# Attention probabilities and values in float32r parts, gates applied by diagonal matrices in the transposes

## The chip, the core and the metric

The kernel runs on one NeuronCore of one Trainium2 chip. TensorE (PE) multiplies, VectorE (DVE), ScalarE (ACT) and GpSimd (POOL) work element by element, and the SyncE queue (SP) issues nearly all transfers. The metric is the device time of one execution in microseconds; less is better.

## What is computed

One layer of a decoder trunk on 512 tokens of 1024 features: RMS norm, one input projection, three groups of heads side by side (six gated DeltaNet heads, six sparse attention heads, a causal pooling), an output projection with a residual, then a squared-ReLU MLP with a residual. The change lies in the sparse attention. Cut to what matters:

```
s   = einsum(q, k)                         # 6 heads, 2 key/value groups, blocks of 128 queries
p_c = masked_softmax(s_cmp);  o_c = p_c @ vc      # compressed keys
o_s = masked_softmax(s_sel) @ vsel                # selected blocks: here all causal keys
o_w = masked_softmax(s_win) @ vwb                 # window of 512: here all causal keys
out = g[..., 0] * o_c + g[..., 1] * o_s + g[..., 2] * o_w
```

With 512 tokens the selection takes every block and the window reaches back over everything, so both branches are plain causal attention with keys and values of their own.

## The kernel before, in words

The program has three stretches. Up to about 245 us, slabs of the input projection run beside the DeltaNet solves and scans. From about 247 to 370 us the attention (`attentions`, L1140) runs beside the first parts of the output projection (`out_gdn`). Then come the last part of the output projection with the second norm (`out_tile`, `x2_norm`, `x2_T`) and the MLP to the end at 732 us.

A Python list of generators (`side_by_side`, L1222) sets the order in which work is written down, and a scheduler that models times orders it again on each engine; the engines then run in that order.

One *unit* of the attention is one head and one of two branches, so there are 12. `probs` (L1092) makes, for each block of 128 queries, the scores: two products of float32r parts (L1100, L1101) and a mask product (L1102); DVE takes the row maximum (L1104), ACT the exponential with its row sum (L1106). When the four blocks are done, DVE makes gate over sum (L1109, L1110) and the four tiles of probabilities are multiplied by it: three on DVE (L1115), the widest on ACT (L1113). `values` (L1117) transposes the ten causal 128 by 128 blocks on PE (L1124) in three groups of four, four and two, copies each group out of PSUM (ACT L1129, DVE L1127 for the second) and multiplies it by the values (L1135), which have 64 columns, in plain float32. A pair of heads shares one PSUM bank: the even head has partitions 0 to 63, the odd one 64 to 127. The compressed branch adds one product per head (L1155). `finish` (L1161) splits the bank into the float32r parts `yTh` and `yTl` (`split_rows`, ACT L148 and DVE L149).

`out_tile` multiplies three products of parts per chunk of features (`mm3`, L143 to L145); each is float32r, 128 by 128 by 512. Its weights are loaded and split into parts by ACT and DVE (`load_wo`, L134 and L135). Chunks 6, 7 and then 0, 1, 2 run beside the attention; 3, 4, 5 (the attention's own) come after it.

`x2_T` (L1247), after the attention, already transposes by a plain float32 product with a diagonal matrix: 4 blocks of tokens by 8 chunks, 32 products.

Of the kernel before, what the change touches and what calls it, by code (L numbers as in the profile page):

```python
# [37 lines left out]
def trunk_kernel(ctx, tc, x, norm_mix, w_in, conv_w, a_log, dt_bias, gdn_norm, nsa_q_norm, nsa_k_norm,  # L38
# [14 lines left out]
    def nm(s):  # L53
        _n[0] += 1
        return f"{s}{_n[0]}"
# [22 lines left out]
    N2 = 25  # L78

    def t2(shape, name, dt=F32):  # L80
        return r2.tile(shape, dt, tag="t", name=nm(name), bufs=N2)

# [307 lines left out]
    halves = [slice(0, 64), slice(64, 128)]  # L390

    XT, Vt = {}, {}
    VC = ctile([96, 2, HD], F32, "VC")
    KCT = ctile([P, 2, 64], F32R, "KCT")
    kr = gdp.tile([P, NT, H, HD], F32, tag="kr", name="kr")
    qr = gdp.tile([P, NT, H, HD], F32, tag="qr", name="qr")
# [186 lines left out]
    def compress_half(a, q):  # L583
# [25 lines left out]
        if a == 0:  # L609
            kp = acc[:, 384:448]  # L610
            for m in range(2):
                PE.matmul(kp[0:64, 0:HD], hh[:, ts(m, 64)], w2[:, m, :], start=(m == 0), stop=(m == 1))
            kcs = cmp_.tile([64, HD], F32, tag="kcs", name=nm("kcs"))
            ss = sml.tile([P, 1], F32, tag="ss1", name=nm("ss"))
            r = sml.tile([P, 1], F32, tag="r1", name=nm("r"))
            S.activation(kcs, kp[0:64, 0:HD], AF.Square, accum_out=ss[0:64])
            V.tensor_scalar(ss[0:64], ss[0:64], 0.5 / HD, 0.5 * EPS, ALU.mult, ALU.add)
            rsqrt(r[0:64], ss[0:64], 1, 64)
            V.scalar_tensor_tensor(kcs, kp[0:64, 0:HD], r[0:64], gk_b[0:64, 0, :], ALU.mult, ALU.mult)
            kx = cmp_.tile([64, 2, P], F32, tag="hid", name=nm("kx"))  # L620
            S.copy(kx[:, 0, 0:HD].bitcast(F32R), kcs)
            S.copy(kx[:, 0, HD:P].bitcast(F32R), kcs)
            V.tensor_tensor(kx[:, 1, 0:HD], kcs, kx[:, 0, 0:HD], ALU.subtract)
            V.tensor_tensor(kx[:, 1, HD:P], kcs, kx[:, 0, 0:HD], ALU.subtract)
            kq = acc[:, 0:128]
            for b in range(2):
                PE.transpose(kq[:, ts(b, 64)], kx[:, b, :], ident[:64, :64])
            S.copy(KCT.rearrange("p k (b n) -> p b k n", b=2), kq[:, 0:128].rearrange("p (b k n) -> p b k n", b=2, k=2))
        else:
            vp = acc[:, 384:512]  # L630
            for rep in range(3):
                for kv in range(2):
# [3 lines left out]
            S.copy(VC, vp[0:96, 0:128].rearrange("p (k d) -> p k d", k=2))  # L636


    PW = ctile([P, 2, P], F32, "PW")
# [41 lines left out]
                G.tensor_tensor(z3, z3, gnh.unsqueeze(1).to_broadcast([P, n // HD, HD]), ALU.mult)  # L681

    def vcopy(b0, pss):
        for b in range(2):
            if b not in Vt:
                Vt[b] = t2([P, 2, 4, HD], "Vt")
            S.copy(Vt[b][:, :, b0:b0 + 2, :], pss[b][:, :, 0:128].rearrange("p i (k d) -> p i k d", k=2))

    def conv_slab(cols):
        fs = {"q": 0, "k": 384, "v": 768, "u": 2718}  # L690
# [354 lines left out]
    wr = ctx.enter_context(pool("wr", 2, side="right"))  # L1045
    nwe = ExitStack()
    nw = nwe.enter_context(pool("nw", 2, side="right"))
    wop = [nwe.enter_context(pool(f"wo{n}", n, side="right")) for n in (4, 6)]
    gd.close()
    fe = ExitStack()  # L1050
    wq = fe.enter_context(pool("wq", 2))


    pn, pt_, pa = banks(0, 1), banks(2, 6), banks(7)

    def cmp_probs(kv):

# [28 lines left out]
        pt = nw.tile([96, T], F32, tag=f"pcT{kv}", bufs=1, name=nm("pcT"))  # L1086
        S.copy(pt, tp[0:96])
        return pt

    BLKS = ([(0, i) for i in range(4)], [(1, i) for i in range(1, 4)] + [(3, 3)], [(2, 2), (2, 3)])  # L1090

    def probs(h, br, out):  # L1092

        kv = h // 3
        kb = 6 + 4 * br + 2 * kv
# [12 lines left out]
            yield 0.11 * (i + 1)  # L1108
        V.reciprocal(sm, sm)  # L1109
        V.tensor_tensor(sm, sm, gate[:, :, 3 * h + 1 + br], ALU.mult)  # L1110
        for i in range(NT):
            if i == 3:
                S.mul(out[i], out[i], sm[:, i:i + 1])  # L1113
            else:
                V.tensor_scalar(out[i], out[i], sm[:, i:i + 1], None, ALU.mult)  # L1115

    def values(acc, h, br, Ps):  # L1117

        a = h % 2
        for b, blks in enumerate(BLKS):  # L1120
            n = len(blks) * P
            tp = pt_()
            for c, (k, i) in enumerate(blks):
                PE.transpose(tp[:, ts(c, P)], Ps[i][:, ts(k, P)], ident)  # L1124
            pt = nw.tile([P, n], F32, tag=f"pt{b}", name=nm("pt"))
            if b == 1:
                V.tensor_copy(pt, tp[:, :n])  # L1127
            else:
                S.copy(pt, tp[:, :n])  # L1129
            yield 0.4  # L1130
            c = 0
            while c < len(blks):
                k, i = blks[c]
                m = sum(1 for x_ in blks if x_[0] == k)
                PE.matmul(acc[halves[a], i * P:(i + m) * P], Vt[k // 2][:, k % 2, 2 * br + h // 3, :],  # L1135
                          pt[:, c * P:(c + m) * P], start=False, stop=(br == 1 and k == 2), skip_group_check=True)
                c += m
            yield 0.4

    def attentions():  # L1140
        last = iter(())
        for pr in range(3):
            hd = (2 * pr, 2 * pr + 1)
            for h in hd:
                if h % 3 == 0:
                    pcT[h // 3] = cmp_probs(h // 3)
            acc = pa()
            for br in range(2):
                for h in hd:
                    Ps = []  # L1150
                    yield from in_turn((probs(h, br, Ps), last))
                    if br == 0 and h == hd[0]:
                        for a, h_ in enumerate(hd):
                            r = slice(32 * (h_ % 3), 32 * (h_ % 3) + 32)
                            PE.matmul(acc[halves[a]], VC[r, h_ // 3], pcT[h_ // 3][r], start=True, stop=False,  # L1155
                                      skip_group_check=True)
                    last = values(acc, h, br, Ps)
                    if br == 1 and h == hd[1]:
                        last = finish(last, pr, acc)
        yield from last  # L1160

    def finish(gen, pr, acc):
        yield from gen
        y_tiles((3 + pr,))
        split_rows(yTh[3 + pr], yTl[3 + pr], acc)
        have.add(("y", 3 + pr))

    pcT = {}


    wo = {}
# [233 lines left out]
```

## Time and profile before

| | us |
|---|---|
| median of 3 runs | 734.62 (733.9 to 736.54) |
| profiled execution, its own time | 734.32 |
| its span in the trace | 732.5 |

A row of the trace gives an instruction's start and how long it was under way. A matmul's row includes its way through the array, which overlaps the next one: what one costs PE is the distance from its start to the start of the next.

### The profile page before, as it was taken

The page shows a single profiled execution, that of the slowest core. Times are in us where ns is not written, and L with a number is a line of the kernel's source. Part 1 is how long each engine was busy: PE and PEld are TensorE (multiplying, and loading weights), DVE is VectorE, ACT ScalarE, POOL GpSimd, SP SyncE. Part 2 cuts the span into 40 slices and gives each one's busy share as a digit, 9 for nine tenths or more (in the row PEclk, how much of TensorE's full clock was granted, in tenths as well). Part 3 has the DMA queues.
Part 4 walks back from the last instruction along what each step waited for, and adds up shares of the span by engine and source line. Part 5 has one row for each costly group of instructions (what it writes and reads, how often), then busy time and mean ns, then how long its engine had stood idle before and what let it go on. Part 6 is the DMA issues. An engine that isn't in the chain of part 4 may idle for free.

```text
span 732.5 us, 13228 instructions
## 1 busy us (share of the span) xinstructions
PE 709.9 (97%) x5147; PEld 567.7 (77%) x5147; DVE 550.1 (75%) x1046; ACT 369.4 (50%) x728; POOL 170.1 (23%) x256
## 2 busy tenths in 40 slices
PE   8999999998999999999999999999999999999997
PEld 6888877886998767666478878888888888888885
DVE  4688998878686588676545798896858688796846
ACT  4456835564663366466525744454544544444430
POOL 5730003312042110000020150404124050403223
PEclk9999999999999999999999999999999999999999
DMA  6233223131410531023001142413142332303103
GB/s 219 60 108 98 75 60 87 31 96 56 118 44 3 214 104 58 2 63 112 0 6 81 58 173 66 165 44 129 58 148 82 115 115 88 133 16 111 58 1 115
DMA packets 49780, 61.67 MB, mean 84 GB/s; under 512 B 5479, under 2 KB 42549, under 8 KB 49718
## 3 DMA queue, kind: packets, MB, share of 16 engines
q1 hardware_dynamic: 48852, 60.64, 26.1%
q8 instruction: 40, 0.66, 0.4%
q10 hardware_dynamic: 866, 0.20, 0.1%
q14 instruction: 22, 0.18, 0.1%
HBM read 58.73 MB, written 2.10 MB: 83 GB/s over the span
## 4 chain that ended last, share of the span: by engine, by line
PE 78%; DVE 13%; issue 2%; ACT 2%; DMA 1%; POOL 1%; SPq 0%; DVEq 0%; ACTq 0%; POOLq 0%
PE ps L143 18%; PE ps L144 18%; PE ps L145 17%; PE ps L429 6%; PE ps L1135 4%; PE ps L800 2%; PE ps L1124 2%; PE ps L1100 1%; PE ps L592 1%; DVE lo L135 1%; PE ps L1101 1%; PE ps L905 1%; DVE bl L1281 1%; DVE lw L135 1%; DMA raw<-in_w_in_dram 1%
## 5 line engine op out<-in xcount | busy, mean ns | idle before, releaser
L144 PE MATMUL ps<-h2l,hw 128*128 128x512 f32 (+1 forms) x280 | 104.7, 375 | 0.1
L145 PE MATMUL ps<-h2h,lw 128*128 128x512 f32 (+1 forms) x280 | 104.3, 374 | 0.0
L143 PE MATMUL ps<-h2h,hw 128*128 128x512 f32 (+1 forms) x280 | 103.8, 374 | 0.0
L143 PE MATMUL ps<-bh,ah 128*128 128x512 f32 x224 | 88.6, 396 | 0.6 <-DVE x L1374 0.6
L1288 POOL TENSOR_TENSOR al<-gF,ah 128x512 fp32r<-128x512 f32 x24 | 37.6, 1568 | 219.3 <-ACT ah L1287 180.2
L144 PE MATMUL ps<-bl,ah 128*128 128x512 f32 x224 | 88.4, 395 | 0.0
L145 PE MATMUL ps<-bh,al 128*128 128x512 f32 x224 | 84.8, 394 | 0.0
L1374 DVE TENSOR_TENSOR x<-ps,x 128x512 f32<-128x512 f32 x112 | 72.5, 680 | 5.8 <-PE ps L145 5.7
L1281 DVE TENSOR_TENSOR bl<-w2r,bh 128x1024 fp32r<-128x1024 f32 x40 | 57.8, 1446 | 6.2 <-ACT bh L1280 6.2
L144 PEld LDWEIGHTS ps<-h2l,hw 128*128 128x128 f32 x280 | 52.6, 188 | 10.3 <-DVE h2l L1252 0.3
L145 PEld LDWEIGHTS ps<-h2h,lw 128*128 128x128 f32 x280 | 52.5, 188 | 10.1
L143 PEld LDWEIGHTS ps<-h2h,hw 128*128 128x128 f32 x280 | 52.2, 188 | 10.1
L1288 POOL TENSOR_TENSOR al<-gS,ah 128x512 fp32r<-128x512 f32 x32 | 53.4, 1685 | 26.0 <-ACT ah L1287 26.0
L135 DVE TENSOR_TENSOR lo<-raw,hi 128x512 fp32r<-128x512 f32 (+1 forms) x76 | 43.3, 593 | 15.5 <-ACT hi L134 11.9
L1280 ACT CAST bh<-w2r 128x1024 fp32r<-128x1024 f32 x40 | 41.7, 1046 | 23.5 <-PE ps L145 23.2
L143 PEld LDWEIGHTS ps<-bh,ah 128*128 128x128 f32 x224 | 42.1, 188 | 11.4 <-ACT ah L1287 0.8
L134 ACT CAST hi<-raw 128x512 fp32r<-128x512 f32 (+1 forms) x76 | 37.0, 518 | 26.8 <-DMA raw<-in_w_in_dram 9.3
L144 PEld LDWEIGHTS ps<-bl,ah 128*128 128x128 f32 x224 | 42.2, 188 | 9.8
L145 PEld LDWEIGHTS ps<-bh,al 128*128 128x128 f32 x224 | 42.1, 188 | 9.9
L135 DVE TENSOR_TENSOR lw<-raw,hw 128x1024 fp32r<-128x1024 f32 x32 | 41.2, 1321 | 6.4 <-ACT hw L134 6.2
L1287 ACT CAST ah<-gS 128x512 fp32r<-128x512 f32 x32 | 19.7, 620 | 51.8 <-DVE gS L1356 24.5
L134 ACT CAST hw<-raw 128x1024 fp32r<-128x1024 f32 x32 | 32.1, 1046 | 24.9 <-PE ps L144 22.6
(364 smaller groups left out, 1674.0 us busy)
## 6 DMA issues: line engine op xcount, KB each, us to landing
raw<-in_w_ffn_dram SPq DMA_DIRECT2D x32, 512.0 KB, 3.8
w2r<-in_w_ffn_dram SPq DMA_DIRECT2D x32, 512.0 KB, 6.4
raw<-in_w_in_dram SPq DMA_DIRECT2D x24, 256.0 KB, 2.9
raw<-in_w_in_dram SPq DMA_DIRECT2D x36, 128.0 KB, 2.5
x<-in_x_dram SPq DMA_DIRECT2D x8, 512.0 KB, 6.0
raw<-in_cmp_w_dram SPq DMA_DIRECT2D x32, 128.0 KB, 2.2
raw<-in_w_out_dram SPq DMA_DIRECT2D x8, 512.0 KB, 4.5
out_dram<-x SPq DMA_DIRECT2D x8, 256.0 KB, 2.0
```

The costliest lines, as they stand in the source:

```text
L134: {"A": S.copy, "V": V.tensor_copy, "G": G.tensor_copy}[e[0]](hi[:, k], r)
L135: {"V": V, "G": G}[e[1]].tensor_tensor(lo[:, k], r, f32v(hi[:, k]), ALU.subtract)
L143: PE.matmul(ps, ah, bh, start=start, stop=False, **kw)
L144: PE.matmul(ps, ah, bl, start=False, stop=False, **kw)
L145: PE.matmul(ps, al, bh, start=False, stop=stop, **kw)
L429: PE.matmul(ps[:, ts(i, 256)], a_[:, k, ts(2 * b + i, P)], w_, start=(k == 0 and n_ == 0 and i == 0), stop=(k == KC - 1 and n_ == 2 and i ...
L1135: PE.matmul(acc[halves[a], i * P:(i + m) * P], Vt[k // 2][:, k % 2, 2 * br + h // 3, :], pt[:, c * P:(c + m) * P], start=False, stop=(br = ...
L1280: S.copy(hi, src)
L1281: V.tensor_tensor(lo, src, f32v(hi), ALU.subtract)
L1287: S.copy(hi, src)
L1288: G.tensor_tensor(lo, src, f32v(hi), ALU.subtract)
L1374: V.tensor_tensor(x2[i][:, cs], acc[bk, t_], x2[i][:, cs], ALU.add)
```

## The change

What it does, part by part:

- Probabilities are no longer multiplied by gate over sum. `probs` makes four diagonal matrices `dg` (ACT, `ident` scaled by `sm`), and the blocks are transposed by a plain float32 product with `dg`, which applies the gate, in place of PE's transposition with `ident`.
- For the first two groups of blocks, probabilities are split into two float32r parts (ACT and DVE), and values are stored as [high | low], 128 columns. Each of the two parts is multiplied by both, so an accumulator has the sum with the high values in partitions 0 to 63 and with the low values in 64 to 127. The third group stays float32 with 64 columns (`Vt[2]`).
- Each head has an accumulator of its own, on banks 7 and 3 in turn. `finish` adds its two halves (ACT copy, DVE addition) and, for the odd head, splits the pair's result from SBUF.
- The compressed values get 128 columns and zero rows for other heads (`VCz`); their probabilities are split too.
- `vcopy` and the compressed values (`VC`) split when they leave PSUM. The pool of common tiles grows from 25 to 27, and the pool `wo6` (weights of chunks 0 to 2) is laid out after the DeltaNet's pool `gd` is closed.

```diff
-    VC = ctile([96, 2, HD], F32, "VC")
+    VC = ctile([96, 2, 2, HD], F32R, "VC")
...
-            S.copy(Vt[b][:, :, b0:b0 + 2, :], pss[b][:, :, 0:128].rearrange("p i (k d) -> p i k d", k=2))
+                S.copy(Vt[i][:, b0:b0 + 2], src)
+            else:
+                split_rows(Vt[i][:, b0:b0 + 2, 0], Vt[i][:, b0:b0 + 2, 1], src)
...
-    wop = [nwe.enter_context(pool(f"wo{n}", n, side="right")) for n in (4, 6)]
+    wop = [nwe.enter_context(pool("wo4", 4, side="right"))]
     gd.close()
+    wop.append(nwe.enter_context(pool("wo6", 6, side="right")))
...
-    pn, pt_, pa = banks(0, 1), banks(2, 6), banks(7)
+    pn, pt_, pa = banks(0, 1), banks(2, 6), banks(7, 3)
...
+        dg = nw.tile([P, NT, P], F32, tag="dgp", name=nm("dg"))
         for i in range(NT):
-            if i == 3:
-                S.mul(out[i], out[i], sm[:, i:i + 1])
-            else:
-                V.tensor_scalar(out[i], out[i], sm[:, i:i + 1], None, ALU.mult)
+            S.activation(dg[:, i], ident, AF.Copy, scale=sm[:, i:i + 1])
+            out[i] = out[i], dg[:, i]
...
-                PE.transpose(tp[:, ts(c, P)], Ps[i][:, ts(k, P)], ident)
-            pt = nw.tile([P, n], F32, tag=f"pt{b}", name=nm("pt"))
-            if b == 1:
-                V.tensor_copy(pt, tp[:, :n])
+                PE.matmul(tp[:, ts(c, P)], Ps[i][0][:, ts(k, P)], Ps[i][1], start=True, stop=True)
+            if b == 2:
+                pt = [nw.tile([P, n], F32, tag=f"pt{b}", name=nm("pt"))]
+                S.copy(pt[0], tp[:, :n])
             else:
-                S.copy(pt, tp[:, :n])
+                pt = [nw.tile([P, n], F32R, tag=f"pt{c}{b}", name=nm("pt")) for c in "hl"]
+                split_rows(pt[0], pt[1], tp[:, :n])
...
-                PE.matmul(acc[halves[a], i * P:(i + m) * P], Vt[k // 2][:, k % 2, 2 * br + h // 3, :],
-                          pt[:, c * P:(c + m) * P], start=False, stop=(br == 1 and k == 2), skip_group_check=True)
+                for p_ in pt:
+                    v_ = Vt[k][:, 2 * br + h // 3]
+                    PE.matmul(acc[0:64 if b == 2 else P, i * P:(i + m) * P],
+                              v_ if b == 2 else v_.rearrange("p c d -> p (c d)"),
+                              p_[:, c * P:(c + m) * P], start=False, stop=(br == 1 and b == 2), skip_group_check=True)
...
+                if br == 0:
+                    for n_, p_ in enumerate(pcT[h // 3]):
+                        PE.matmul(acc, VCz[:, h], p_, start=n_ == 0, stop=False, skip_group_check=True)
...
+        S.copy(o[a], acc[halves[1 - h % 2]])
+        V.tensor_tensor(o[a], acc[a], o[a], ALU.add)
+        if h % 2:
+            y_tiles((3 + h // 2,))
+            split_rows(yTh[3 + h // 2], yTl[3 + h // 2], o)
```

The order moves at three places that matter here. PE, the last unit, before: transposes (`P`), value products (`pt`, `Vt`; output 64 partitions), then the output projection.

```order
L1124 MATMUL ps_5541<-ident,P_5517 128x128 x2
L1135 MATMUL ps_5240<-pt_5538,Vt_4003 64x512
L1124 MATMUL ps_5550<-ident,P_5502 128x128
L1124 MATMUL ps_5550<-ident,P_5517 128x128
L1135 MATMUL ps_5240<-pt_5546,Vt_4003 64x384
L1135 MATMUL ps_5240<-pt_5546,Vt_4005 64x128
L1135 MATMUL ps_5240<-pt_5553,Vt_4005 64x256
L143 MATMUL ps_5576<-hwo_5250,yTh_4993 128x512
```

And now (line numbers are those of the changed kernel, L1130 the transposition by `dg`, L1144 the value product):

```order
L1130 MATMUL ps_5680<-dg_5658,P_5650 128x128 x2
L1144 MATMUL ps_5523<-pt_5674,Vt_4004 128x512
L1144 MATMUL ps_5523<-pt_5675,Vt_4004 128x512
L1144 MATMUL ps_5523<-pt_5685,Vt_4007 128x384
L1130 MATMUL ps_5693<-dg_5658,P_5633 128x128
L1130 MATMUL ps_5693<-dg_5658,P_5650 128x128
L1144 MATMUL ps_5523<-pt_5686,Vt_4007 128x384
L1144 MATMUL ps_5523<-pt_5685,Vt_4012 128x128
L1144 MATMUL ps_5523<-pt_5686,Vt_4012 128x128
L1144 MATMUL ps_5523<-pt_5696,Vt_4010 64x256
L143 MATMUL ps_5721<-hwo_5346,yTh_5018 128x512
```

Three of the value products stand twice, once per part, and only the last has 64 output partitions. In the whole program the visits of PE to value products with 64 output columns (runs of such rows, those of the compressed values included) fall from 29 to 12.

ACT, the end of the attention, before: multiplication of the widest probabilities, two copies, the split of the result.

```order
L1106 ACTIVATE P_5517,sm_5471<-ps_5511,mx_5515 128x512
L1129 COPY pt_5530<-ps_5527 128x256
L1113 ACTIVATE P_5517<-P_5517,sm_5471 128x512
L1129 COPY pt_5538<-ps_5533 128x512
L1129 COPY pt_5553<-ps_5550 128x256
L148 CAST yTh_5556<-ps_5240 128x512
```

And now:

```order
L1112 ACTIVATE P_5650,sm_5599<-ps_5644,mx_5648 128x512
L1133 COPY pt_5666<-ps_5663 128x256
L1119 ACTIVATE dg_5658<-ident,sm_5599 128x128 x4
L148 CAST pt_5674<-ps_5669 128x512
L148 CAST pt_5685<-ps_5680 128x512
L1133 COPY pt_5696<-ps_5693 128x256
L1176 COPY o_5594<-ps_5523 64x512
L148 CAST yTh_5701<-o_5594 128x512
```

Four diagonals stand in place of one wide multiplication, both large groups are cast here, and a copy stands ahead of the result's cast.

ACT, the weights of chunks 0 to 2 (`hwo`) beside the scans (`vb`, whose last row is the scan's last copy), before: the first of the three casts.

```order
L909 COPY vb<-ps_3288 64x3x64 x2
L134 CAST hwo_4826<-raw_4828 128x1024
L1106 ACTIVATE P_4605,sm_4598<-ps_4599,mx_4603 128x128
L1106 ACTIVATE P_4628,sm_4598<-ps_4622,mx_4626 128x256
L1113 ACTIVATE P_4588<-P_4588,sm_4533 128x512
L134 CAST hwo_4832<-raw_4834 128x1024
```

And now, three scan steps later, behind the scan's last copy:

```order
L913 COPY vb<-ps_3408 64x3x64
L1112 ACTIVATE P_4931,sm_4924<-ps_4925,mx_4929 128x128
L923 ACTIVATE sq_4448<-vb 128x384
L1119 ACTIVATE dg_4912<-ident,sm_4816 128x128 x4
L148 CAST yTh_3242<-ps_4378 128x128
L1112 ACTIVATE P_4948,sm_4924<-ps_4942,mx_4946 128x256
L134 CAST hwo_4877<-raw_4879 128x1024
```

These weights now lie where tiles of the scan were, and wait for its end.

## Rows read from the trace of the kernel before

**Rows 1.** Page, parts 1 and 4: busy engines; the last-ending chain by engine.

```profile
PE 709.9 (97%) x5147; PEld 567.7 (77%) x5147; DVE 550.1 (75%) x1046; ACT 369.4 (50%) x728; POOL 170.1 (23%) x256
...
PE 78%; DVE 13%; issue 2%; ACT 2%; DMA 1%; POOL 1%; SPq 0%; DVEq 0%; ACTq 0%; POOLq 0%
```

**Rows 2.** Stretches: length, busy PE, PEld, DVE, ACT, POOL (count), granted clock, DMA.

```profile
247.00:270.00 23.00, 21.79 (x180) 15.01 (x180) 20.59 (x55) 13.21 (x29) 4.62 (x7) 0.93 0.62 223
...
345.00:372.00 27.00, 25.91 (x125) 14.42 (x124) 12.79 (x32) 13.42 (x35) 0.00 (x0) 1.00 0.00 1
355.00:370.00 15.00, 13.91 (x65) 7.16 (x65) 7.25 (x19) 7.59 (x20) 0.00 (x0) 1.00 0.01 2
```

**Rows 3.** PE groups by line and shape, 235 to 380 us.

```profile
L1124 PE MATMUL ps<-ident,P 128*128 128x128 f32 x120 | 19.8, 283 | 0.3 <-ACT pcT L1087 0.2
L1135 PE MATMUL ps<-pt,Vt 128*64 128x512 f32 x24 | 12.9, 618 | 0.4 <-ACT pt L1129 0.3
```

**Rows 4.** Timeline of PE: start, us, engine, line, shape, count.

```profile
351.29 0.28 PE L1101 MATMUL ps<-XT,XT 128*128 128x128 f32 x1
351.40 0.23 PE L1102 MATMUL ps<-negb,identb 128*128 128x128 bf16 x1
...
352.99 0.61 PE L1124 MATMUL ps<-ident,P 128*128 128x128 f32 x4
353.53 0.65 PE L1135 MATMUL ps<-pt,Vt 128*64 128x256 f32 x2
354.11 0.66 PE L1124 MATMUL ps<-ident,P 128*128 128x128 f32 x4
...
354.78 0.34 PE L1101 MATMUL ps<-XT,XT 128*128 128x384 f32 x1
354.95 0.23 PE L1102 MATMUL ps<-negb,identb 128*128 128x128 bf16 x1
355.12 1.07 PE L1135 MATMUL ps<-pt,Vt 128*64 128x512 f32 x2
356.12 0.44 PE L1124 MATMUL ps<-ident,P 128*128 128x128 f32 x2
```

**Rows 5.** Timeline of PE after the attention: output projection, then diagonal products.

```profile
383.24 0.39 PE L145 MATMUL ps<-hwo,yTl 128*128 128x512 f32 x1
383.47 1.95 PE L1247 MATMUL ps<-dg,x 128*128 128x128 f32 x16
385.17 0.48 PE L143 MATMUL ps<-hwo,yTh 128*128 128x512 f32 x1
```

**Rows 6.** Line L1247: count, min/median/max ns.

```profile
L1247 PE MATMUL ps<-dg,x x64: 270/275/377, 383.5 to 401.2; 128*128 128x128 f32 x64
```

**Rows 7.** Timeline: the cast of chunk 2's weights, the compressed values' products.

```profile
265.80 1.05 ACT L134 CAST hwo<-raw 128x1024 fp32r<-128x1024 f32 x1 [0.52 <-DMA raw<-in_w_out_dram]
...
265.91 1.07 PE L1155 MATMUL ps<-pcT,VC 32*64 32x512 f32 x4
```

**Rows 8.** ACT groups, 235 to 380 us.

```profile
L1113 ACT ACTIVATE P<-P,sm 128x512 f32<-128x512 f32 x12 | 8.6, 720 | 2.4 <-DVE sm L1110 2.3
```

**Rows 9.** Timeline of ACT: scaled copies of 128x128.

```profile
384.56 2.17 ACT L1250 ACTIVATE h2h<-ps,vT 128x128 fp32r<-128x128 f32 x8 [2.42 <-PE ps L1247]
```

**Rows 10.** Timeline: the last unit, from gate over sum to the output projection.

```profile
364.12 0.18 DVE L1109 RECIPROCAL sm<-sm 128x4 f32<-128x4 f32 x1 [0.84 <-ACT P L1106]
...
364.53 0.88 DVE L1115 TENSOR_SCALAR P<-P,sm 128x128 f32<-128x128 f32 x3
...
369.54 0.50 PE L143 MATMUL ps<-hwo,yTh 128*128 128x512 f32 x1
...
369.64 0.59 ACT L148 CAST yTh<-ps 128x512 fp32r<-128x512 f32 x1 [1.07 <-PE ps L1135]
...
370.26 0.69 DVE L149 TENSOR_TENSOR yTl<-ps,yTh 128x512 fp32r<-128x512 f32 x1 [3.16 <-ACT yTh L148]
...
371.03 0.40 PE L143 MATMUL ps<-hwo,yTh 128*128 128x512 f32 x1
```

More of the change, by code (lines that the diff above doesn't have):

```diff
@@ L77, in trunk_kernel @@
     r2 = ctx.enter_context(pool("r2", 1))
-    N2 = 25
+    N2 = 27
     def t2(shape, name, dt=F32):
@@ L635, in compress_half @@
                                   w2[:, m, :], start=(m == 0), stop=(m == 1))
-            S.copy(VC, vp[0:96, 0:128].rearrange("p (k d) -> p k d", k=2))
+            split_rows(VC[:, :, 0], VC[:, :, 1], vp[0:96, 0:128].rearrange("p (k d) -> p k d", k=2))
     PW = ctile([P, 2, P], F32, "PW")
@@ L683, in vcopy @@
     def vcopy(b0, pss):
-        for b in range(2):
-            if b not in Vt:
-                Vt[b] = t2([P, 2, 4, HD], "Vt")
-            S.copy(Vt[b][:, :, b0:b0 + 2, :], pss[b][:, :, 0:128].rearrange("p i (k d) -> p i k d", k=2))
+        for i in range(NT):
+            src = pss[i // 2][:, i % 2, 0:128].rearrange("p (k d) -> p k d", k=2)
+            if i not in Vt:
+                Vt[i] = t2([P, 4, HD], "Vt") if i == 2 else t2([P, 4, 2, HD], "Vt", F32R)
+            if i == 2:
+                S.copy(Vt[i][:, b0:b0 + 2], src)
+            else:
+                split_rows(Vt[i][:, b0:b0 + 2, 0], Vt[i][:, b0:b0 + 2, 1], src)
     def conv_slab(cols):
@@ L1085, in cmp_probs @@
             PE.transpose(tp[0:96, ts(i, P)], pc[:, i].rearrange("p g n -> p (g n)"), ident)
-        pt = nw.tile([96, T], F32, tag=f"pcT{kv}", bufs=1, name=nm("pcT"))
-        S.copy(pt, tp[0:96])
+        pt = [nw.tile([96, T], F32R, tag=f"pcT{c}{kv}", bufs=1, name=nm("pcT")) for c in "hl"]
+        split_rows(pt[0], pt[1], tp[0:96])
         return pt
@@ L1110, in probs @@
         V.tensor_tensor(sm, sm, gate[:, :, 3 * h + 1 + br], ALU.mult)
+        dg = nw.tile([P, NT, P], F32, tag="dgp", name=nm("dg"))
         for i in range(NT):
-            if i == 3:
-                S.mul(out[i], out[i], sm[:, i:i + 1])
-            else:
-                V.tensor_scalar(out[i], out[i], sm[:, i:i + 1], None, ALU.mult)
+            S.activation(dg[:, i], ident, AF.Copy, scale=sm[:, i:i + 1])
+            out[i] = out[i], dg[:, i]
     def values(acc, h, br, Ps):
-        a = h % 2
         for b, blks in enumerate(BLKS):
@@ L1140, in attentions, with finish @@
     def attentions():
+        G.memset(f32v(VCz), 0.0)
+        for h in range(H):
+            r = slice(32 * (h % 3), 32 * (h % 3) + 32)
+            S.copy(VCz[r, h], f32v(VC[r, h // 3]).rearrange("p c d -> p (c d)"))
         last = iter(())
[L1142 to L1146, printed above, removed]
+        for h in range(H):
+            if h % 3 == 0:
+                pcT[h // 3] = cmp_probs(h // 3)
             acc = pa()
             for br in range(2):
[L1149 to L1159, printed above, removed]
+                Ps = []
+                yield from in_turn((probs(h, br, Ps), last))
+                if br == 0:
+                    for n_, p_ in enumerate(pcT[h // 3]):
+                        PE.matmul(acc, VCz[:, h], p_, start=n_ == 0, stop=False, skip_group_check=True)
+                last = values(acc, h, br, Ps)
+            last = finish(last, h, acc)
         yield from last
-    def finish(gen, pr, acc):
+    def finish(gen, h, acc):
         yield from gen
-        y_tiles((3 + pr,))
-        split_rows(yTh[3 + pr], yTl[3 + pr], acc)
-        have.add(("y", 3 + pr))
+        a = halves[h % 2]
+        if h % 2 == 0:
+            os_[0] = nw.tile([P, T], F32, tag="o", bufs=1, name=nm("o"))
+        o = os_[0]
+        S.copy(o[a], acc[halves[1 - h % 2]])
[3 more added lines that the diff above has]
+            split_rows(yTh[3 + h // 2], yTl[3 + h // 2], o)
+            have.add(("y", 3 + h // 2))
+    os_ = {}
     pcT = {}
+    VCz = nw.tile([96, H, P], F32R, tag="VCz", bufs=1, name="VCz")
     wo = {}
```

## The prediction

> **What bounds the kernel now.** I read the page first: PE is busy for 97% of the span and has 78% of the chain that ended last [rows 1]. A matmul's row overlaps the next one's, so busy time alone says little; what an instruction costs is the distance to the next start. I then read the stretches: in the attention, 247 to 372 us, DVE and ACT are busy about half to nine tenths of the time, while PE is nearly always so, also in the last 15 us, which have no output projection beside them: 13.9 us of PE, 7.6 us of ACT [rows 2]. So the attention is bound by what PE starts, and a microsecond added to or taken from PE's starts moves the end by about as much. At its end ACT and DVE come in too, since one unit's steps then wait for each other. The granted clock is 0.93 in the first stretch and 1.00, the level of 2.4 GHz, in the later ones shown [rows 2]; the change's instructions lie nearly all behind the first, so I cost them at that level.
>
> **The transposes.** A transposition of 128 columns starts 0.11 us after the one before: four take 0.61 us with 0.28 us for the last alone, so three steps are 0.33 us [rows 4, 3]. There are 120 of them [rows 3]: 13.2 us. Now each is a plain float32 product with a diagonal. The same form is in the kernel already, in x2_T: 32 products in the code, 64 instructions in the trace [rows 6], so each is two, and 16 of them take 1.95 us with 0.275 for the last, a step of 0.112 us [rows 5, 6]. For 120 products that is 240 x 0.112 = 26.9 us: **+13.7 us**. The gate, which costs PE nothing in this form, is paid by that second instruction.
>
> The Trainium skill, page TensorE: Matmul & The Clock Gate, section Terms, says that the transpose mode makes a float32 transposition four times as fast; by it each product with a diagonal costs 0.44 us, and the sum would be 25.9 us higher than mine. The rows of L1247 say two, and I go by them.
>
> **The value products.** Before, each is plain float32 with 64 output columns and two instructions (24 rows of 512 columns for 12 units [rows 3]). The pair of 512 columns at 355.12 is followed after 1.00 us, the pair of 256 at 353.53 after 0.58 us [rows 4]. The difference, 0.42 us for 512 columns, is 0.82 ns per column and instruction, and 0.16 us remain of each pair, whatever its length. Ahead of it the last of four transposes starts at 352.99 + 0.33 and its successor 0.21 us later instead of 0.11 [rows 4]: 0.10 us more. So a visit to products of 64 output columns costs 0.26 us beside its columns. The 12 units have 1280 columns each, twice: 2560 x 12 x 0.82 ns = 25.2 us, and 29 visits are 7.5 us: 32.7 us in all.
>
> Now, three of four products are float32r with 128 output columns, one instruction per part. At 512 columns they follow each other after 0.23 us (383.24 to 383.47) [rows 5], at 384 after 0.17, at 128 after 0.11 [rows 4]: 24 x (0.23 + 0.17 + 0.11) = 12.2 us. The third group stays as it was: 12 x 512 x 0.82 ns = 5.0 us, with 12 visits at 0.26 = 3.1 us. That is 20.3 us: **-12.4 us**. Compressed values: four instructions in 1.0 us before [rows 7], so 3.0 us for 12; now 12 float32r products of 512, 2.8 us: **-0.2 us**.
>
> PE in all: 13.7 - 12.4 - 0.2 = **+1.1 us**. What the values win, the transposes take back.
>
> **The end of the attention.** Before, the cast of the last result starts at 369.64 and takes 0.59 us, and its first reader starts at 371.03 [rows 10]; six products with chunks 3 and 4 fill the time between, and the order has the same six now. So 0.8 us are free there. Now a copy (0.59), an addition on DVE (0.69, as L149) and the cast (0.59) follow each other: 1.87 us against 1.39, **+0.5 us**; the DVE part of the split, 0.69 more [rows 10], is needed only six further products later and costs nothing while those stand ahead of its reader.
>
> **The last units.** Gate over sum is ready at 364.53; three multiplications take 0.88 us on DVE beside 0.72 us on ACT [rows 8, 10]. Now ACT makes four diagonals in turn. Eight scaled copies of that size take 2.17 us on ACT, 0.27 each [rows 9]; four are 1.1 us: +0.2. Eight transposes (two groups) are 8 x 0.11 = 0.9 us longer, the value products behind them about 1.1 us shorter, and the low part of the second group comes a cast and a subtraction (0.59 + 0.69) after its transposes, where one copy stood. I take +0.4 for the last unit. Per unit ACT does 4 x 0.27 + 0.59 (second group) + half of 0.59 (half a result's copy) more and 0.72 less: +1.2 us. In 355 to 370 us, where ACT is half busy [rows 2], that lies in the chain from maximum to exponential for two units, 2.4 us; half of it is behind PE's longer transposes: **+1.2 us**. Bounds for both: 0 (all behind PE) and +4.
>
> **What I cost at nothing.** The splits in vcopy, VC and VCz: a few casts of 0.3 us beside projection slabs that keep PE fed; without that cover +1.5. The two accumulators: a head's result is taken while the next head runs. DVE loses 36 multiplications and gains as many microseconds in subtractions. The weights of chunks 0 to 2: their casts (1.05 us each [rows 7]) now stand behind the scan's last copy, but their products also need results of that scan; if they are late, three casts, +3. No DMA is added or moved on SP's queue; the memset on POOL stands between scan products that wait for the solves anyway.
>
> **Sum.** 1.1 + 0.5 + 0.4 + 1.2 = +3.2 us on the profiled execution's 734.32: 737.5. That execution lies 0.3 us below the median of the runs, so against the median the change is +2.9 us, 0.4%. Half a per cent, 3.7 us here, is about what a measurement tells from no change.
>
> **The rivals.**
> - *Covered:* the ends of units hide behind PE and only PE's +1.1 is left, or a little less, if visits cost more than I read. 734 to 736. For: PE is at 97%. Against: the last units, where PE waits. 0.23.
> - *ACT becomes the bound:* ACT gets 12 x 1.2 = 14 us more, in order, with diagonals that wait for DVE ahead of the next unit's exponentials, and PE waits for those. If half of it is exposed, that is +7; it decides where an exponential is later than the end of PE's work before it. 740 to 746. For: DVE is at 90% in the first stretch, so its part of the chain is tight there [rows 2]. Against: in the last 27 us ACT is busy for 13.4, and four units add 4.8 [rows 2]. 0.17.
> - *A shorter chain:* transposes no longer wait for multiplied probabilities, only for a diagonal. The first diagonal is there about 0.3 us after the gate, where the multiplied tiles take 0.88; 12 units x 0.5 us = 6 us less, and PE's sum +1.1: 729.5. It decides only where PE waits at that place. For: L1115 is in the chain of the last unit. Against: PE has other products between, and the third and fourth diagonals are later than before. 0.12.
> - *Four passes:* a product with a diagonal takes as long as four transposes, 0.44 us: 120 x (0.44 - 0.224) = 26 us more than forecast, 763. The 64 rows for 32 products in L1247, the same form, speak against it [rows 6]. 0.02. This is the factor that the Trainium skill's page on TensorE gives, cited above.
> - That the change does not do what it says: the order shows the products by dg and the parts, so nothing is kept for that.
>
> **How the numbers follow.** My forecast, PE about even and the ends longer, has 0.46, with 735.5 to 740. Slower by over 0.5% (above 738.3) is two fifths of it, all of the ACT case and of the four passes: 0.38. Faster by over 0.5% (below 730.9) is most of the shorter chain: 0.11, and the rest is the same: 0.51. The range, 732 to 743, leaves out the shorter chain's lower end and the upper end of the ACT case.
>
> **What would show it.** In the profile after: 240 instructions on the transposes' line, steps of 0.11 us; value products at 0.23 us for 512 columns; the last value product 2 to 4 us later than 369 us relative to the first scores, and the MLP's length unchanged. If the attention's length is unchanged or shorter, the ends were covered; if PE's idle time ahead of transposes is above some 5 us with ACT as its releaser, ACT is the bound. I would be wrong in the main term if a diagonal product took one instruction: then the change would be 13 us faster than I say.

## The result and the profile after

The changed kernel takes 737.85 us (median of 20 runs, 736.04 to 742.6) against 734.54 for the kernel before (20 runs): ratio 1.0064, 95% interval 1.0043 to 1.0084. The forecast, 737.5, is 0.35 us away. Four of its terms can be read in the trace of the changed kernel, and they did not come out as well as their sum.

The page, parts 1 and 4, to set beside [rows 1]:

```profile
PE 709.6 (97%) x5267; PEld 585.5 (80%) x5267; DVE 552.7 (75%) x1037; ACT 387.5 (53%) x792; POOL 167.5 (23%) x257
...
PE 73%; DVE 16%; ACT 4%; DMA 4%; issue 3%; POOL 1%; SPq 0%; ACTq 0%; DVEq 0%; POOLq 0%
```

PE has the 120 instructions more that the diagonals need; DVE, DMA and ACT have 3, 3 and 2 points more of the chain that ended last, and PE 5 fewer. That PE's busy share stands at 97% in both says nothing, as a matmul's row overlaps the next one's.

PE's groups in the attention by shape (instructions, busy us, mean ns, idle time ahead and its releaser); they answer to [rows 3], and the 240 instructions for 120 transposes to [rows 6]:

```profile
L1130 PE MATMUL ps<-dg,P 128*128 128x128 f32 x240 | 34.4, 282 | 0.2 <-ACT dg L1119 0.2
L1144 PE MATMUL ps<-pt,Vt 128*128 128x512 f32 x24 | 10.1, 449 | 1.3 <-DVE pt L149 1.0 <-ACT pt L148 0.2
L1144 PE MATMUL ps<-pt,Vt 128*128 128x384 f32 x24 | 8.3, 367 | 0.1
L1144 PE MATMUL ps<-pt,Vt 128*64 128x256 f32 x24 | 7.7, 404 | 0.1
L1144 PE MATMUL ps<-pt,Vt 128*128 128x128 f32 x24 | 4.0, 248 | 0.0
L1165 PE MATMUL ps<-pcT,VCz 96*128 96x512 f32 x12 | 4.7, 444 | 0.0
```

The step of the transposes' instructions is in PE's timeline; ten start within 1.14 us, 0.114 us each:

```profile
354.13 1.38 PE L1130 MATMUL ps<-dg,P 128*128 128x128 f32 x10
355.27 0.71 PE L145 MATMUL ps<-hwo,yTl 128*128 128x512 f32 x2
```

The weight loads of the value products wait for the low parts, which come a cast and a subtraction after the transposes (view of the waits: us in total, times, longest):

```profile
PEld ps L1144 <- DVE pt L149: 2.4, 4, 1.0
```

The stretches, to set beside [rows 2]: ACT has 18.6 of 27 us in the last one where it had 13.4, DVE 13.2 against 12.8, and the granted clock is 1.00 in both.

```profile
247.00:270.00 23.00, 22.32 (x217) 17.59 (x217) 18.71 (x60) 13.49 (x41) 3.02 (x5) 1.00 0.29 116
...
345.00:372.00 27.00, 25.91 (x162) 20.50 (x161) 13.21 (x29) 18.56 (x55) 0.00 (x0) 1.00 0.00 1
```

The end of the attention (timeline), to set beside [rows 10]: copy, addition and cast follow each other, and PE waits 0.47 us for the cast.

```profile
372.25 0.58 ACT L1176 COPY o<-ps 64x512 f32<-64x512 f32 x1 [0.73 <-PE ps L1144]
...
372.86 0.69 DVE L1177 TENSOR_TENSOR o<-ps,o 64x512 f32<-64x512 f32 x1 [2.33 <-ACT o L1176]
...
373.59 0.62 ACT L148 CAST yTh<-o 128x512 fp32r<-128x512 f32 x1 [0.76 <-DVE o L1177]
...
374.26 0.50 PE L143 MATMUL ps<-hwo,yTh 128*128 128x512 f32 x1 [0.47 <-ACT yTh L148]
```

**Where the time went.** From the first scores to the first product of x2_T the two profiles have 136.3 us (247.1 to 383.5) and 142.6 us (244.3 to 386.8): +6.3. From there to the end of the last product on PE it is 345.35 and 344.75 us: 0.6 less. The stretch ahead of the first scores is 2.9 us shorter in the profile after, but the two traces are already 3.1 us apart at the 50th product on PE, in work that the change does not touch, and the profiles of all kernels below lie between 243.6 and 249.6 us there, whichever attention follows. Totals of single executions differ by that much, so the medians decide on totals, and the stretch from first scores to x2_T is used to see the attention alone.

To see what that stretch is made of, I added up the distances between neighbouring starts on PE. *Work* is a usual distance for each source line and shape (the lower quartile at full clock over all these kernels), *half* what is lost on top while the granted clock is 0.50, the level of 1.2 GHz, and *wait* all that is left, a switch between forms included. With other ways to form the usual distance, work and wait move against each other by 1 to 3 us; the stretch and the half do not depend on it much. One profile each, us:

```
kernel                              stretch  work   wait  half
before                               136.3  104.8   30.2   1.3
the change                           142.6  111.4   31.2   0.0
parts, plain transposes              137.1   98.4   33.2   5.5
diagonals alone                      147.7  118.3   28.2   1.3
change, diagonals on DVE             143.1  111.4   31.6   0.0
parts, no scaling                    133.5   97.5   34.5   1.5
parts, products with identity        141.2  111.1   30.0   0.0
parts, products in two heads         135.8  102.4   33.4   0.0
parts, weights' low part on POOL     143.6   98.1   42.1   3.4
parts, scaling on POOL               134.0   98.1   33.1   2.7
parts, third group 128 columns       135.4   97.7   32.2   5.4
parts, one score product less        136.2   90.5   40.0   5.7
parts, POOL and 128 columns          130.5   96.2   34.3   0.0
```

For the change: work +6.6, wait +1.0, half -1.3. So most of the cost is in PE's own starts, not in the chain at the ends of the units. The switches into products of 64 columns, 3.2 us before and 1.6 after, are in wait, so the other waits grew by some 2.6 us. The profile of the parts alone is the slowest of its twelve runs (736.64 us).

### The profile page after: what moved, and what is told of

It reads as the page before. It is cut to its first block, busy times and chain, and to the rows that moved or that the text cites. A ratio compares the mean times of both kernels' runs of the same rounds, so it can differ in the third digit from the quotient of the medians.

```text
span 735.2 us, 13523 instructions
## 1 busy us (share of the span) xinstructions
PE 709.6 (97%) x5267; PEld 585.5 (80%) x5267; DVE 552.7 (75%) x1037; ACT 387.5 (53%) x792; POOL 167.5 (23%) x257
## 4 chain that ended last, share of the span: by engine, by line
PE 73%; DVE 16%; ACT 4%; DMA 4%; issue 3%; POOL 1%; SPq 0%; ACTq 0%; DVEq 0%; POOLq 0%
PE ps L143 17%; PE ps L144 17%; PE ps L145 17%; PE ps L429 4%; PE ps L1130 3%; PE ps L1144 3%; PE ps L804 2%; DMA raw<-in_w_in_dram 2%; DMA raw<-in_w_out_dram 1%; DVE lo L135 1%; DVE lwo L135 1%; DVE bl L1298 1%; PE ps L592 1%; PE ps L1106 1%; PE ps L237 1%
## 5 line engine op out<-in xcount | busy, mean ns | idle before, releaser
L1305 POOL TENSOR_TENSOR al<-gF,ah 128x512 fp32r<-128x512 f32 x24 | 35.6, 1485 | 227.8 <-ACT ah L1304 188.4
L1391 DVE TENSOR_TENSOR x<-ps,x 128x512 f32<-128x512 f32 x112 | 73.1, 682 | 11.4 <-PE ps L145 11.2
L1305 POOL TENSOR_TENSOR al<-gS,ah 128x512 fp32r<-128x512 f32 x32 | 54.0, 1706 | 18.6 <-ACT ah L1304 17.3
L134 ACT CAST hi<-raw 128x512 fp32r<-128x512 f32 (+1 forms) x76 | 37.0, 518 | 30.1 <-DMA raw<-in_w_in_dram 13.6
L143 PEld LDWEIGHTS ps<-bh,ah 128*128 128x128 f32 x224 | 42.1, 188 | 11.4 <-ACT ah L1304 0.9
L145 PEld LDWEIGHTS ps<-bh,al 128*128 128x128 f32 x224 | 42.1, 188 | 9.7
L144 PEld LDWEIGHTS ps<-bl,ah 128*128 128x128 f32 x224 | 42.1, 188 | 9.6
L135 DVE TENSOR_TENSOR lw<-raw,hw 128x1024 fp32r<-128x1024 f32 x32 | 39.1, 1254 | 11.3 <-ACT hw L134 11.3
L1304 ACT CAST ah<-gS 128x512 fp32r<-128x512 f32 x32 | 19.8, 621 | 42.1 <-DVE gS L1373 24.5
```

Of the source, the lines that this page charges most:

```text
L134: {"A": S.copy, "V": V.tensor_copy, "G": G.tensor_copy}[e[0]](hi[:, k], r)
L135: {"V": V, "G": G}[e[1]].tensor_tensor(lo[:, k], r, f32v(hi[:, k]), ALU.subtract)
L143: PE.matmul(ps, ah, bh, start=start, stop=False, **kw)
L144: PE.matmul(ps, ah, bl, start=False, stop=False, **kw)
L145: PE.matmul(ps, al, bh, start=False, stop=stop, **kw)
L1305: G.tensor_tensor(lo, src, f32v(hi), ALU.subtract)
```

## The experiments

Each ran five rounds beside the kernel before. Ratios are to that kernel; multiplied by its 734 us they give the differences in the text. The four groups of runs were on different chips. A difference between two changed kernels has the errors of both ratios: against the parts alone it is known to some 2.5 us either way, and where a difference below is not larger than that, it is called unclear.

**1. The change again, its two halves apart, and the diagonals on another engine.** Theory: PE's starts set the attention, so the diagonals cost their second instruction and the parts alone gain what the forecast said. Rival: the diagonals' load on ACT is the cost.

The change, repeated:

> The changed kernel again, beside the runs below on the same chip. Theory (PE: the diagonal products cost about what the value products save, and the ends of the units are longer): 1.004 to 1.008 of before. Rivals expect the same.

738.89 us, ratio 1.0079 (1.0051 to 1.0108). The stretch is 142.6 us, as in the first profile, so that measure repeats to 0.1.

Parts alone, transposes as before:

```diff
-            S.activation(dg[:, i], ident, AF.Copy, scale=sm[:, i:i + 1])
-            out[i] = out[i], dg[:, i]
+            if i == 3:
+                S.mul(out[i], out[i], sm[:, i:i + 1])
+            else:
+                V.tensor_scalar(out[i], out[i], sm[:, i:i + 1], None, ALU.mult)
...
-                PE.matmul(tp[:, ts(c, P)], Ps[i][0][:, ts(k, P)], Ps[i][1], start=True, stop=True)
+                PE.transpose(tp[:, ts(c, P)], Ps[i][:, ts(k, P)], ident)
```

> The change with its transposes undone: probabilities are multiplied by the gate as before (three on DVE, one on ACT) and transposed by PE's transposition with ident; parts, banks and finish stay as in the change. Theory: PE loses 120 instructions of 0.112 us, 13.7 us less than the change, of which one or two come back as DVE's multiplications: 724 to 728 us, 0.986 to 0.991 of before. Rival ACT (the diagonals and casts on ACT bind): ACT loses 15.3 us of diagonals and gets 8.6 back, a gain of 3 to 5 us: 733 to 735. Rival ends (only the longer chains of finish and parts cost): no gain, 736 to 739.

733.31 us, ratio 0.9998 (0.9972 to 1.0023). Better than the change by some 6 us, but no better than before: the theory missed by 5 to 9 us, and the time lies in the range of the rival ACT.

Diagonals alone, in the kernel before:

```diff
+        dg = nw.tile([P, NT, P], F32, tag="dgp", name=nm("dg"))
...
-                PE.transpose(tp[:, ts(c, P)], Ps[i][:, ts(k, P)], ident)
+                PE.matmul(tp[:, ts(c, P)], Ps[i][0][:, ts(k, P)], Ps[i][1], start=True, stop=True)
```

> Before with the diagonal products alone: probabilities not multiplied, diagonals on ACT, transposes as plain products; values stay float32 with 64 columns, pairs on one bank. Theory: PE gets 13.7 us, less about two for the multiplications that no longer stand in the chain: 745 to 749, 1.014 to 1.020. Rival ACT: ACT gets 6.7 us, half of it exposed: 736 to 738. Rival ends: the chain is not longer: 734 to 735.

745.19 us, ratio 1.0165 (1.0121 to 1.021): +12 us, as said, and +11.4 in the stretch.

The change with the diagonals made by DVE (`V.tensor_scalar(dg[:, i], ident, sm[:, i:i + 1], None, ALU.mult)`):

> The change with its 48 diagonals made by DVE in place of ACT: PE has the same instructions. Theory: PE binds, so within 2 us of the change, 736 to 740. Rival ACT: 15 us less on ACT: 728 to 733. Rival ends: within 1 us of the change.

739.69 us, ratio 1.0079 (1.0045 to 1.0112), the same as the change. Forty-eight diagonals cost ACT 15.3 us or DVE 11.0, and the time doesn't care which. ACT alone as the cost falls with this, although it had the right range for the parts alone. The rival of the ends, which this run doesn't tell from the theory, had missed both halves.

So the halves do not add: alone they give -0.2 and +12.1 us, together +5.8. The bookkeeping shows how. Added to the kernel before, the diagonals bring +13.5 of work and -2.0 of wait. Added to the parts they bring +13.0 of work, -2.0 of wait, and -5.5 of half. The parts alone bring -6.4 of work, +3.0 of wait, +4.2 of half. Here is the place of that half (stretches of the parts alone; length, busy PE, PEld, DVE, ACT, POOL, granted clock, DMA):

```profile
289.00:293.40 4.40, 2.67 (x16) 1.67 (x14) 4.22 (x19) 4.40 (x13) 0.00 (x0) 1.00 0.00 0
293.40:307.00 13.60, 12.63 (x45) 10.26 (x44) 12.05 (x33) 6.59 (x16) 1.00 (x1) 0.50 0.40 116
```

and the same in the repeated change:

```profile
289.00:293.40 4.40, 3.51 (x20) 2.19 (x20) 4.20 (x14) 4.40 (x10) 0.00 (x0) 1.00 0.16 35
293.40:307.00 13.60, 11.79 (x68) 8.85 (x68) 12.84 (x37) 8.87 (x29) 1.00 (x1) 1.00 0.45 143
```

DVE and ACT are full from 289 to 293.4 in both. In the parts alone PE has 16 instructions in that time, then runs at half clock for 13.6 us; in the change it has 20 and the clock stays. The windows are the same in time and not in work: the first scores are at 248.9 us in the one and 245.1 in the other. Two theories follow. CLOCK: the parts alone lose their gain to the half clock. DVE/ACT: the vector engines, full here, take it back as waits.

**2. Four edits of the parts alone that tell CLOCK from DVE/ACT.**

The scaling left out (the four lines with `sm` above):

> The kernel with the parts and transposes (plain transposes, the other two parts of the change kept), with the scaling of the probability blocks left out as well: the results lack the softmax sums and gates of the two large branches, and 48 multiplications go from DVE and ACT. PE's instructions stay the same. Theory CLOCK (the parts alone gained nothing because PE, without the diagonal products, falls to the half clock for some 14 us around 293 us): 730 to 734 us, granted clock over the runs still under 0.992. Rival DVE/ACT (these engines bound the attention once PE is relieved): 722 to 728 us.

729.67 us, ratio 0.996 (0.9936 to 0.9985): 2.8 us better than the parts alone, just above the errors. That is between the two ranges. The median granted clock of the runs is 0.990, under 0.992 as CLOCK said. The table doesn't put the gain under wait: against the parts alone, wait is 1.3 us longer and half 4.0 us shorter. So this run speaks for the vector engines' load as a cause, but not for shorter waits of PE as the way it acts.

Products with the identity, so that PE has the change's work and DVE and ACT keep the multiplications (120 transposes of two instructions each; the 240 of the expectation are the instructions):

```diff
-                PE.transpose(tp[:, ts(c, P)], Ps[i][:, ts(k, P)], ident)
+                PE.matmul(tp[:, ts(c, P)], Ps[i][:, ts(k, P)], ident, start=True, stop=True)
```

> Normalised probabilities as in the kernel with plain transposes, but each of the 240 transposes is one fp32 product with the identity: PE does the work of the change, DVE and ACT that of the other. Theory CLOCK: 13.7 us more PE time, some 7 us of it returned by the clock: 738 to 742 us, granted clock over the runs 0.99 to 1.00, no half-clock stretch at 290 to 310 us. Rival DVE/ACT: PE's longer products lie beside the busy vector engines: 733 to 736 us.

736.87 us, ratio 1.0064 (1.0036 to 1.0091), 4.8 us above the parts alone and not told apart from the change (1.0079). The time lies between the ranges too, while CLOCK's signs came (median clock 0.993, no half clock in the attention). Two things follow. The gate inside the product gives nothing back that a run can show; the price is the float32 product itself, here with the identity:

```profile
L1131 PE MATMUL ps<-ident,P 128*128 128x128 f32 x240 | 34.5, 282 | 0.7 <-DVE pt L149 0.5 <-DVE P L1121 0.2
```

And 12.7 us more of work on PE cost 4.8 us of time; in the two profiles 3.2 us of wait and 5.5 of half went away.

Such products in heads 1 and 2 alone (`if h in (1, 2)` around the two forms):

> Plain transposes except in heads 1 and 2 of six (the units around 270 to 310 us), which have products with the identity: 80 products, +4.6 us on PE. Theory CLOCK: the half-clock stretch at 293 to 307 us goes (some 7 us back), 730 to 732 us, and granted clock above that of plain transposes. Rival (the dip is an accident of single executions, or DVE bounds): 734 to 738 us.

734.06 us, ratio 1.002 (0.9992 to 1.0049). The half clock is gone from this stretch, and the median clock of the runs is 0.993 against 0.984, as CLOCK said, but the time is not below that of the parts alone (1.6 us above, unclear): CLOCK's 730 to 732 missed; the median is just at the rival's lower end. In the single profiles the stretch from first scores to x2_T is 1.3 us shorter than in the parts alone. Nor is a thin PE enough for the fall. Here too PE was busy for little of 4.4 us, and the clock stayed at 1.00 behind it:

```profile
294.70:299.10 4.40, 2.55 (x15) 1.71 (x13) 3.89 (x15) 1.98 (x7) 0.00 (x0) 1.00 0.72 209
299.10:313.00 13.90, 12.19 (x67) 9.79 (x68) 12.40 (x32) 6.99 (x18) 1.01 (x1) 1.00 0.27 85
```

The low parts of the output weights on POOL (`load_w(..., "wo", "AG")` for `"AV"`):

> Plain transposes, with the low parts of the output weights computed on POOL in place of DVE (8 of 128x1024): DVE loses some 9 us in the attention. Theory CLOCK: PE's thin stretch at 289 to 294 us came from waits for DVE and for these weights; if PE is fed there the clock holds and 725 to 729 us result; if the weights then come later still, 732 to 736. Rival DVE/ACT: the attention gets shorter by part of the 9 us whatever the clock does: 726 to 731 us, with the clock still under 0.992.

741.04 us, ratio 1.0122 (1.007 to 1.0174), the worst of these four. Its rows:

```profile
L135 POOL TENSOR_TENSOR lwo<-raw,hwo 128x1024 fp32r<-128x1024 f32 x8 | 19.0, 2384 | 39.0 <-ACT hwo L134 38.0 <-DMA raw<-in_w_out_dram 1.0
...
L1131 PE MATMUL ps<-ident,P 128*128 128x128 f32 x120 | 21.1, 291 | 6.2 <-DVE P L1121 3.8 <-DVE r L104 1.4 <-ACT pt L1134 0.9
```

A subtraction that takes DVE 1.22 us takes POOL 2.38, and PE's transposes wait 6.2 us where those of the parts alone wait 1.4. Wait rises to 42.1 us. Every range missed. Why DVE's multiplications (L1121) then come so late was not tried.

**3. Less work for one engine at a time.** Now WAITS: whatever is taken from PE comes back in part as waits for the others.

The 36 multiplications of DVE on POOL (`G.tensor_scalar` for `V.tensor_scalar`):

> The parts with plain transposes, the 36 multiplications of DVE (13.3 us there) put on POOL, which is nearly idle in the attention. Theory WAITS (what PE saves is taken back by waits for DVE, ACT and the output weights; leaving the scaling out gave 3.6 us): 730 to 732 us, unless POOL's longer multiplication (its 128x512 operations take 1.6 us) delays the transposes: then 734 to 737. Rival (DVE's load is no cause, the time without scaling came from the shorter chain before the transposes): 733 to 737 us.

730.25 us, ratio 0.9961 (0.9936 to 0.9986): within WAITS' range, and as good as leaving the scaling out (2.7 us better than the parts alone, just above the errors). But the mechanism of WAITS does not show: in the table wait is as long as in the parts alone (33.1 and 33.2), and half is 2.8 us shorter.

128 columns for the third group's values, the second half zero:

```diff
-                Vt[i] = t2([P, 4, HD], "Vt") if i == 2 else t2([P, 4, 2, HD], "Vt", F32R)
+                Vt[i] = t2([P, 4, 2, HD], "Vt") if i == 2 else t2([P, 4, 2, HD], "Vt", F32R)
+                if i == 2:
+                    G.memset(Vt[i][:, :, 1], 0.0)
...
-                    PE.matmul(acc[0:64 if b == 2 else P, i * P:(i + m) * P],
+                    PE.matmul(acc[:, i * P:(i + m) * P], v_.rearrange("p c d -> p (c d)"),
```

> The parts with plain transposes; the third group's 24 fp32 products also have 128 columns, with a zero half, so that no product of the attention has 64 columns: 12 visits fewer at about 0.26 us, 3.1 us of PE time, and no work more for DVE or ACT (the half is zeroed once on POOL). If PE bounds the attention: 729.5 to 731 us. Theory WAITS: a third of it at most, 732 to 733.5 us.

730.4 us, ratio 0.9965 (0.9944 to 0.9987): 2.4 us better than the parts alone, no more than the errors, where the forecast's 0.26 us per visit gives 3.1. PE's bound hits and WAITS misses: this saving seems to come through, how much of it is unclear.

One score product less:

```diff
-            PE.matmul(sc[:, 0:n], XT[h][:, ts(i, P)], XT[kb + 1][:, 0:n], start=False, stop=False)
```

> The parts with plain transposes, with the second of the two products of every score block left out (48 products of 128 to 512 columns, 7 us of PE time; the results lack the low part of the keys), DVE and ACT unchanged. If PE bounds the attention: 725 to 727 us. Theory WAITS: at most a third to a half of it comes back, 729.5 to 732 us, and the trace shows longer waits of PE in the attention.

728.95 us, ratio 0.9937 (0.9908 to 0.9965): 4.5 us for 7, and with its errors the whole 7 is not ruled out. Neither range holds it. In its profile work is 7.9 us lower and wait 6.8 higher (that execution, at 732.39 us, is the slowest of its twelve, so it shows the direction rather than the size).

**4. The two edits that helped, together.**

> The two earlier edits together: plain transposes, the scaling on POOL, and 128 columns for the third group's products. Apart they gave 3.1 and 2.9 us against the parts with plain transposes. If their gains add: 727 to 728 us. Theory WAITS (less PE work lays waits for the vector engines bare, and each edit removes partly the same waits): 728.5 to 730 us. Rival (both gains are the start-up and clock of other executions): 730 to 733 us.

726.21 us, ratio 0.9907 (0.9875 to 0.9939): below both kernels, by 0.9% against before and, ratio to ratio, 1.6 to 1.7% against the change. That is below the range for adding the two gains and below that of WAITS, which missed; 6.7 us against the parts alone and the sum of 5.1 are not told apart. In the table 5.5 us of the gain in the stretch stand under half, 2.2 under work, and wait is 1.1 us longer. Its transposes are plain ones and its clock is 1.00 where the parts alone had 0.50:

```profile
289.00:293.40 4.40, 3.53 (x15) 1.73 (x14) 4.40 (x15) 4.09 (x11) 2.74 (x3) 1.00 0.57 136
293.40:307.00 13.60, 12.05 (x68) 9.33 (x67) 11.93 (x36) 6.35 (x19) 5.87 (x5) 1.00 0.32 110
```

The multiplications take POOL two to more than three times as long as DVE, beside work that hardly needs POOL. Groups of POOL in the last kernel:

```profile
L1123 POOL TENSOR_SCALAR P<-P,sm 128x384 f32<-128x384 f32 x12 | 16.0, 1334 | 0.0
L1123 POOL TENSOR_SCALAR P<-P,sm 128x256 f32<-128x256 f32 x12 | 12.1, 1009 | 0.0
L1123 POOL TENSOR_SCALAR P<-P,sm 128x128 f32<-128x128 f32 x12 | 8.2, 682 | 57.2 <-ACT pcT L148 19.8 <-DVE sm L1118 11.1 <-PE ps L1133 8.3
```

and of DVE in the parts alone:

```profile
L1121 DVE TENSOR_SCALAR P<-P,sm 128x384 f32<-128x384 f32 x12 | 5.0, 413 | 0.0
L1121 DVE TENSOR_SCALAR P<-P,sm 128x256 f32<-128x256 f32 x12 | 4.2, 347 | 0.0
L1121 DVE TENSOR_SCALAR P<-P,sm 128x128 f32<-128x128 f32 x12 | 4.1, 339 | 0.4
```

**What stays open.** How much of the missing gain of the parts is the clock's and how much is waits. For the clock: the bookkeeping above, where the runs that improved on the parts by less scaling on DVE have less half and not less wait, and the ratios, by which diagonals cost 12.1 us on the kernel before (median granted clock 0.991, 0.990 with them) and 5.9 on the parts (0.984, with them 0.999). Against it: the run with products in two heads, and the runs of the parts alone among themselves, where five at 0.99 have a median of 733.4 us and seven at 0.978 to 0.985 one of 732.5. Neither side is clean. The seven fall into four of 731.9 to 732.5 us and three of 735.0 to 736.6, and a run's mean clock doesn't say where it was low: in the profile of the parts alone it was also low ahead of the attention, at 177 and at 235 us, where that of the repeated change had 1.00:

```profile
177.30:184.10 6.80, 6.57 (x54) 5.78 (x53) 4.85 (x17) 2.66 (x8) 2.78 (x5) 0.50 0.05 9
235.30:238.70 3.40, 3.40 (x30) 3.23 (x27) 2.53 (x6) 0.19 (x1) 2.62 (x6) 0.51 0.00 0
```

No run changed the clock and nothing else.

## Why the prediction was right

**The sum was right, and one of its terms, the value products, was not.** Against the median of before it said +2.9 us; measured +3.3 by the medians, +4.7 by the ratio (and +5.8 by the ratio of the second series; its interval goes from 3.7 to 7.9).

- *Transposes, +13.7:* right. 240 instructions, 27.0 us from start to start against my 26.9, and diagonals alone cost 12 us. By the Trainium skill's factor of four (page TensorE: Matmul & The Clock Gate, section Terms) it would have been some 26 us more; the trace disagrees: two instructions of 0.112 us stand for one of 0.109, a factor of two. That rival is dead.
- *Value products, -12.4:* the term that failed, and in its second half. Before, my 32.7 us hold: from start to start the lines of the value products have 29.3 us, and the entries, 0.09 to 0.14 us on the instruction ahead of each of the 29 visits, are 3.2 more, on the lines of those instructions. A mask product is such an instruction. Its successor starts 0.04 us after it in the rows below, and 0.17 us after it where that is a value product (354.95 to 355.12 [rows 4]).

```profile
316.95 0.23 PE L1102 MATMUL ps<-negb,identb 128*128 128x128 bf16 x1
316.99 0.48 PE L143 MATMUL ps<-hwo,yTh 128*128 128x512 f32 x1
```

  After, I said 20.3 us, and it is 23.8 (23.1 on the lines, 0.7 of entries elsewhere): -8.7 and not -12.4. Of the 3.5 us, 1.7 stand in three steps of 0.97, 0.73 and 0.73 us at 512 columns, where 0.23 was my price. There PE waits for the low part, which comes a cast and a subtraction after the transposes and which I had only in the ends of units; one of the three is the step from 363.87 to 364.60:

```profile
363.87 0.50 PE L1144 MATMUL ps<-pt,Vt 128*128 128x512 f32 x1
364.60 0.67 PE L1144 MATMUL ps<-pt,Vt 128*128 128x512 f32 x2 [0.22 <-DVE pt L149]
```

  The rest lies in some twenty steps about 0.1 us longer than the rows I had read; why is not shown.
- *PE's sum, +1.1:* with compressed values (3.4 us after, not 2.8) the three lines came to +6.4, from 47.2 to 53.5 us; the entries that stand on lines other than these three fall from 2.5 to 0.6 us, so with them it is +4.5.
- *Finish, +0.5:* right; PE waits 0.47 us for the cast at 374.26.
- *Last units, +0.4 and +1.2:* not to be seen apart. Wait grew by 1.0 us over the whole stretch, 2.6 without the switches, of which the three steps above are 1.7, and diagonals on DVE gave the same time. ACT as the bound falls with them.
- *What made up for the 3.4 us that PE's sum was short:* in the profiles the attention is 6.3 us longer where I had +3.2, and the total comes out at +2.9 because the start-up is 2.9 us shorter in this execution and what follows the attention 0.6; 1.3 us of half clock that before has and the change has not is in the 6.3. In the medians the gap is 3.3, by the ratios 4.7 and 5.8, so part of my sum's closeness is luck.
- *"A microsecond added to or taken from PE's starts moves the end by about as much":* the step of the first part that failed, and the larger finding. Added to the kernel before, 13.5 us of PE's work moved the end by 12. In the kernel with parts, where PE has 98 and not 105 us of work in the stretch, 12.7 us more moved it by 4.8. Taking work from PE there gave 4.5 us for 7 and 2.4 for 3.1, where the errors allow the whole, and DVE's 13 us of multiplications, moved away, gave 2.7. So PE is not the only bound there; how much of the difference is other engines' waits and how much the half clock (5.5 us in the one profile) is open, as said above.
- *The rivals:* covered (734 to 736) is just missed: PE's +1.1 was +4.5, and of the ends only the finish shows by itself. The shorter chain did not show: products with the identity, which wait for multiplied probabilities, are no slower than the change.

## What to carry to other kernels

A scaling that rides in a float32 transpose is not free on PE: here it turned one instruction into two, and an idle POOL did the same multiplication for less, though each took it two to three times as long. Before a change with two halves is kept, each half is worth running alone: here one half cost 12 us by itself and the other nothing, and the second, with its scaling moved to POOL and its last 64-column products gone, was 7 us faster than the kernel before. And "PE bound" was true of one kernel and not of the next: once PE's work is cut, what a further microsecond is worth has to be measured again, with the granted clock and the other engines' load in the stretch where PE is thin beside it.

## What the runs showed of the hardware

- In the kernel before, PE once ran products of 64 output columns of two heads side by side: in the row at 332.93, which is named by its first shape, two instructions of 256 columns and two of 512 take 1.01 us, where alone the pairs take 0.58 and 1.00. It saves 0.4 us, in one of 27 places, and the trace of the change has no such place.

```profile
332.93 1.08 PE L1135 MATMUL ps<-pt,Vt 128*64 128x256 f32 x4
333.94 0.66 PE L1124 MATMUL ps<-ident,P 128*128 128x128 f32 x4
```

- Going into products of 64 output columns made the step of the instruction ahead 0.09 to 0.15 us longer, at 29 places before and 12 after; where PE also waited, more.
- POOL took 1.33 us to multiply 128x384 by a scalar per partition and 2.38 us to subtract 128x1024, against DVE's 0.41 and 1.22. Put on POOL, the first went with a gain of 2.7 us and the second with a loss of 9; in the second PE's transposes waited 6.2 us.
- The granted clock fell to 0.50 for 13.6 us behind 4.4 us in which PE was busy for 2.67, and stayed at 1.00 behind 4.4 us with 3.51 and, in the run with products in two heads, with 2.55. What decides it is not shown. The Trainium skill, page TensorE: Matmul & The Clock Gate, section Part 4: PE-mode transpose, says that transposes do not count as a busy PE the way products do. The last kernel, with plain transposes throughout and 1.00 in the attention, shows that this alone does not decide it here.
